# One token-ordered buffer for branch B's results, one load per merge, whole-tile loads of queries and keys, and earlier gate weights, in a hybrid encoder layer

## The chip, the cores and the metric

The kernel runs on one core of a Trainium2 chip. The metric is the device time of one execution in microseconds (us); lower is better. TensorE (PE) does the matmuls, VectorE (DVE), ScalarE (ACT) and GpSimd (POOL) the rest; SyncE (SP) and POOL issue the DMA transfers, which 16 DMA engines carry out. Everything is float32; a matrix product is made of several matmuls of high and low parts (`hi`, `lo`), so that TensorE is busy nearly all the time.

## The reference

1280 tokens (1024 of a sample, 256 of a prompt, as two sequences) pass through one encoder layer of width 1024, here with the RMS norms, reshapes and the final norm left out:

```python
z = h @ w_in                       # queries, keys, values of branches A and B, and 2 x 1024 gate logits
gates = sigmoid(z[..., o6:] + b_gate).reshape(b, S, 2, D_MODEL)
o_a = _banded_attention(qa, ka, va, 128, 1, rel_bias[:, :8], sink)     # 8 heads, 2 key heads
# branch B: three dilations (1, 4, 16), 4 heads each
for gi, (window, dil) in enumerate(B_GROUPS):
    o, lse = _banded_attention(_to_residues(qb), _to_residues(kb), _to_residues(vb), window // (2 * dil), dil, ...)
    outs.append(_from_residues(o, dil)); lses.append(_from_residues(lse, dil))
alpha = softmax(stack(lses), axis=0)          # over the three dilations, per token and head
o_b = sum(alpha[..., None] * stack(outs))
merged = gates[:, :, 0] * (o_a @ w_branch_a) + gates[:, :, 1] * (o_b @ w_branch_b)
x = x + merged @ w_out
return x + square(relu(rmsnorm(x) @ w_up)) @ w_down
```

A "residue" of a dilation `dil` is every `dil`-th token. The attention of a dilation runs over residues, so its results come out in residue order.

## The kernel before, in words

The tokens are 10 tiles of 128, 8 of the sample (`NS` = 1024 tokens) and 2 of the prompt (`NP` = 256). The kernel has stages one after the other: input projections, with branch B's attention woven in (to about 550 us); branch A's attention with the gate logits of the sample's leftovers and the prompt and with branch B's merge (about 555 to 706 us); branch projections, gating and output projection; the MLP. The change touches the end of the first and the whole of the second. Each engine runs its instructions in the order in which the program gives them (`manual_schedule`); nothing is reordered at run time, and an instruction that waits holds up all behind it on its engine. SP's list of DMAs, too, is in program order.

*Branch B's results.* `leave` (L580 to L603) copies an attention step's results, their negated maxima and their sums into rows of `ROW` = 132 numbers (528 bytes), and POOL's DMAs put them into three DRAM buffers, `scr_b[g]` for dilation `g`, ordered by residue. For each of the 10 merges (a pair of token tiles `t`, `t+1` and a head pair `i`), `load_rows` (L1142 to L1158) brings the rows of 256 tokens and three dilations into a tile `r` of 128 partitions; since the buffers are ordered differently and a merge wants the same tokens of all three, it takes 8 SP DMAs for a sample pair and 6 for a prompt pair. `alpha_steps` computes the softmax weights on DVE and ACT, `merge` the weighted sum on DVE, `turn_merged` transposes the result for the next product and puts the tokens back in order.

*Branch A.* A unit `u` (0 to 3) is a head pair. `load_unit(u)` loads keys (`kk`, the sample's, 4 KB a row; `kp`, the prompt's, 1 KB a row) for every second unit, and queries (`q`, and by `load_prompt` `qp`) for each. Keys and queries lie in DRAM with 64 rows for a head; the tile has them in both halves of the 128 partitions (`HALVES`): the keys twice the same, the queries two heads. Each half is a DMA of its own from 64 rows. The loop over 40 tiles `(u, t)` (written in pairs, `i` and `j`, at its call site) does for each: scores on PE into a bank `sc` (L1059, L1060), bias and maximum on DVE, exponentials on ACT, transposes, values on PE (`pv`, L1103), one or two steps of `fill` (gate logits, L191 on PE) and, by `merge_steps`, as many steps of the ten merges as keep `done[1]` at 50*(i+j-1)/35. Unit `u+1` is loaded when unit `u` starts. The rows of merge `n`+2 are loaded in the course of merge `n`.

*Gate weights.* `fetch` (L221) loads the next raw weight tile (`raw`, 512 KB), `prepare` splits it into `whi` (ACT) and `wlo` (DVE); the weights are consumed by `fill`. `entering` (L626 to L641) is a generator of which a step is done at each step of the last projections: it fetches the first raw tile, loads bias and unit 0, fetches the second raw tile, loads four parts of the normalized input that had been put by (`h21`: `hhi`, `hlo` from `scr_h`), and prepares the first weight. Among these on SP's list stand stores `scr_g<-z` of finished gate logits.

Of the kernel before, what the change touches and what calls it, by code (L numbers as in the profile page):

```python
# [10 lines left out]
F32 = mybir.dt.float32  # L11
# [85 lines left out]
def encoder_kernel(  # L97
# [28 lines left out]
    def slot(name, shape=(P, D), dt=F32):  # L126
        return slots.tile(list(shape), dt, name=name, tag="m", bufs=N_M)
# [90 lines left out]
    def fetch():  # L218
        src, shape, _ = specs[len(raws)]
        raws.append(wslot("raw", shape))  # L220
        nc.sync.dma_start(raws[-1], src)  # L221
# [49 lines left out]

    NH = AH + 3 * BH

    scr_b = [dram.tile([T, 2, ROW], F32, name=f"scr_b{g}_") for g in range(3)]
    scr_o = [dram.tile([P, AH * HD], F32, name=f"scr_o{t}") for t in range(NT)]
    scr_x = [dram.tile([P, D], F32, name=f"scr_x{t}") for t in range(NT)]

# [130 lines left out]

    shared = {}

    def load_unit(u):

        st = {}
        g = u // 2
        if u == 0:
            shared["kp"] = slot("kp", (P, 4, NP), F32R)
        if u % 2 == 0:
            kk = [slot("kk", (P, NS), F32R) for _ in range(2)]
            for i in range(2):
                for r in HALVES:  # L420
                    nc.sync.dma_start(kk[i][r, :].bitcast(F32), scr_ka[i, g, :, :NS])
                    nc.sync.dma_start(shared["kp"][r, 2 * g + i, :].bitcast(F32), scr_ka[i, g, :, NS:])
            shared["k"] = [Pair(kk[i], shared["kp"][:, 2 * g + i, :]) for i in range(2)]
        st["q"] = [Pair(slot("q", (P, NS), F32R), None) for _ in range(2)]
        for h in range(2):
            for a in range(2):
                nc.sync.dma_start(st["q"][h].s[HALVES[a], :].bitcast(F32), scr_qa[u][a, h, :, :NS])
        if u:
            load_prompt(u, st)
        else:  # L430
            shared["v"] = [slot("va", (P, 8, P)), None]
            nc.sync.dma_start(shared["v"][0],
                              scr_v[:NS, 512 : 512 + P].rearrange("(t p) c -> p t c", p=P))
        st["k"], st["v"] = shared["k"], shared["v"]
        return st

    def load_prompt(u, st):
        for h in range(2):
            st["q"][h].p = qslot("qp", (P, NP), F32R)
            for a in range(2):  # L440
                nc.sync.dma_start(st["q"][h].p[HALVES[a], :].bitcast(F32), scr_qa[u][a, h, :, NS:])
        if not u:
            shared["v"][1] = qslot("vp", (P, 2, P))
            nc.sync.dma_start(shared["v"][1], scr_v[NS:, 512 : 512 + P].rearrange("(t p) c -> p t c", p=P))
# [46 lines left out]
    def attention_b(make):  # L491
# [100 lines left out]
        def leave(j, pv, st):  # L592
            o = make("o", (P, 4, ROW), n=2)
            for b, (g, i, tiles) in enumerate(steps[j]):
                c, nt = 2 * b, len(tiles)
                if b == 0 or nt != len(steps[j][0][2]) or nt == 1:
                    m = 4 if b == 0 and nt == len(steps[j][1][2]) == 2 else nt
                    nc.scalar.activation(o[:, c : c + m, : 2 * HD],
                                         pv[:, P * c : P * (c + m)].rearrange("p (x c) -> p x c", c=P), AF.Copy)
                    nc.gpsimd.tensor_copy(o[:, c : c + m, 2 * HD :], st[:, c : c + m, :])  # L600
                for x, (t, (pieces, _, _)) in enumerate(tiles):
                    for p0, nq, qa, _ in pieces:
                        nc.gpsimd.dma_start(scr_b[g][qa : qa + nq, i, :], o[p0 : p0 + nq, c + x, :])  # L603

        load(0)
        yield
# [19 lines left out]
    def entering():  # L626

        nonlocal unit0
        fetch()
        yield  # L630
        bias0 = load_bias(0, wslot)
        yield
        unit0 = load_unit(0), bias0
        yield
        fetch()
        for i in range(2):
            h21[i] = slot("hhi", (P, 2, 512), F32R), slot("hlo", (P, 2, 512), F32R)
            for j in range(2):
                nc.sync.dma_start(h21[i][j].bitcast(F32), scr_h[i][:, j])
        prepare()  # L640
        yield  # L641

# [227 lines left out]
    if True:  # L870
# [157 lines left out]
            b, p = pair(b, p, PAIRS[j], PAIRS[j + 1] if j + 1 < len(PAIRS) else None, hooks, tick)  # L1028
        run(att_b)
        flush(True)  # L1030
    first_part.close()


# [2 lines left out]
    if True:  # L1036
# [101 lines left out]
        def load_rows(i, t):  # L1138

            r = rows_b[i, t] = slot("r", (P, 2, 3, ROW))  # L1142
            for j in range(2):
                if t < 8:
                    a = P // 8 * (t + j)
                    nc.sync.dma_start(r[:, j, 0, :], scr_b[0][P * (t + j) : P * (t + j + 1), i, :].rearrange(
                        "(q m) c -> m q c", m=8))
                    rows = scr_b[1][:NS, i, :].rearrange("(r q m) c -> m r q c", r=4, m=2)[:, :, a : a + 16]
                    for m in range(2):
                        nc.sync.dma_start(r[64 * m : 64 * m + 64, j, 1, :], rows[m])  # L1150
                    nc.sync.dma_start(r[:, j, 2, :], scr_b[2][:NS, i, :].rearrange(
                        "(r q) c -> r q c", r=8)[:, a : a + 16])
                    continue
                nc.sync.dma_start(r[:, j, 0, :], scr_b[0][P * (t + j) : P * (t + j + 1), i, :].rearrange(
                    "(q m) c -> m q c", m=2))
                for g in (1, 2):
                    nc.sync.dma_start(r[:, j, g, :], scr_b[g][NS:, i, :].rearrange(
                        "(r q) c -> r q c", r=2)[:, 64 * j : 64 * j + 64])  # L1158

        alphas = {}  # L1160

# [33 lines left out]
        def merges_of(seq):  # L1195
            load_rows(*seq[0])
            yield
            load_rows(*seq[1])
            for _ in range(5):
                yield  # L1200
            yield from alpha_steps(*seq[0])
            for n, x in enumerate(seq):
                now = merge(*x)
                next(now)
                coming = alpha_steps(*seq[n + 1]) if n + 1 < len(seq) else iter(())
                next(coming, None)
                yield
                next(now)
                yield
                if n + 2 < len(seq):  # L1210
                    load_rows(*seq[n + 2])
                next(now)
                yield
                next(coming, None)
                yield
# [5 lines left out]
    if True:  # L1221
# [5 lines left out]
        def turn_merged(t, tag="sc"):  # L1227

            if t in (0, 4, 8):
                ob_hi.block(t // 4)  # L1230
                ob_lo.block(t // 4)
            ps = bank(tag)
            for j in range(2):
                nc.tensor.transpose(ps[:, P * j : P * j + P], merged[t // 4][:, t % 4, P * j : P * j + P], ident)
            k = 8 if t < 8 else 2
            parts = []
            for j in range(2):
                hi, lo = (x.at(j, P * t, P).rearrange("p (q m) -> p q m", m=k) for x in (ob_hi, ob_lo))
                parts.append((hi, lo, ps[:, P * j : P * j + P].rearrange("p (m q) -> p q m", m=k)))
            banks_t["b", t] = parts  # L1240
            for hi, _, src in parts:
                nc.scalar.activation(hi, src, AF.Copy)
# [56 lines left out]
        for i in range(0, len(order) + 4, 2):  # L1299
            for j in range(2):  # L1300
                if i < len(order):
                    u, t = order[i + j]
                    if t == 0 and u < 3:
                        units[u + 1] = load_unit(u + 1), load_bias(u + 1, lambda name, shape: a3(name, shape, 2))
                    if i >= 36:
                        turn_merged(i + j - 36, "mm")
                    scores(u, t)
                    if j == 0 and i > 2:
                        values_of(*order[i - 4 : i - 2])
                    if i >= 36:  # L1310
                        weights_b = prepare_steps() if j == 0 else weights_b
                        next(weights_b, None)
                        low_b(i + j - 36)
                if i >= len(order) and j == 0:
                    values_of(*order[i - 4 : i - 2])
                if 0 < i < len(order) + 2:
                    transposes(*order[i + j - 2])
                if i < len(order):
                    exponentials(*order[i + j])
                merge_steps(i, j)  # L1320
                steps_of(fill, 2 if i > len(order) - 2 or j and i > 30 else 1)
            if i == 38:
                load_o(0)
                load_o(1)
# [602 lines left out]
```

## Time and profile before

| what | value |
|---|---|
| median of 3 runs (lowest to highest) | 1716.57 us (1714.93 to 1716.98) |
| the profiled execution | 1717.32 us, of which its span in the trace 1715.5 us |
| mean granted TensorE clock | 0.992 of full speed |
| PE busy in the span | 1679.1 us (98%) |
| DVE, ACT, POOL busy | 986.2 us (57%), 727.1 us (42%), 436.3 us (25%) |
| share of the 16 DMA engines taken by the hardware queue q1 / by POOL's software queue q0 | 42.3% / 4.3% |

How to read what follows: times are us from the span's start. "PE L1059 MATMUL sc<-kk,q" is a matmul of line 1059 that writes `sc` and reads `kk` and `q`. In brackets behind an instruction stands how long its engine had been idle and what released it. A view by stretches ("windows") gives for each stretch the busy time and the number of instructions of PE, its weight loads, DVE, ACT and POOL, then the granted clock, the busy share of the 16 DMA engines and GB/s.

### The profile page before, as it was taken

What the parts mean: (1) busy time and instruction counts of PE and PEld (TensorE: products, weight loads), DVE (VectorE), ACT (ScalarE), POOL (GpSimd) and SP (SyncE); (2) the same over time, 40 slices, a digit from 0 to 9 for tenths busy, and PEclk for the clock granted to TensorE, in tenths of its full rate; (3) what the DMA queues carried; (4) which work ended last, traced back from release to release, by engine and by line L of the source; (5) the groups of instructions that cost most, each with busy time, mean ns of one, the idle gap of its engine ahead of it and who ended that gap; (6) DMA issues with size and microseconds to landing.
All of it is one profiled execution on the core that took longest, in us unless ns stands there. A gap on an engine that the chain in (4) does not pass through costs nothing.

```text
span 1715.5 us, 26529 instructions
## 1 busy us (share of the span) xinstructions
PE 1679.1 (98%) x9952; PEld 1428.6 (83%) x9952; DVE 986.2 (57%) x1675; ACT 727.1 (42%) x1550; POOL 436.3 (25%) x401
## 2 busy tenths in 40 slices
PE   7999999999999988999999999999999999999998
PEld 6898888888887877888888888888887888888886
DVE  6734554554442566566568555554547776667575
ACT  6232543544442555635266433333334333333345
POOL 0210122121111121100100264555556332314140
PEclk9999999999999999999999999999999999999999
DMA  7315666664536752727012434443446844633333
GB/s 240 122 50 126 167 177 190 186 188 127 151 121 190 200 153 75 260 90 277 25 74 74 155 117 128 157 133 116 143 157 231 292 131 157 210 115 117 117 117 123
DMA packets 233624, 256.35 MB, mean 149 GB/s; under 512 B 30447, under 2 KB 164035, under 8 KB 233368
## 3 DMA queue, kind: packets, MB, share of 16 engines
q1 hardware_dynamic: 224024, 229.05, 42.3%
q0 software_dynamic: 8384, 23.51, 4.3%
q10 hardware_dynamic: 1088, 2.10, 0.3%
q8 instruction: 79, 1.29, 0.3%
q14 instruction: 49, 0.40, 0.1%
HBM read 169.10 MB, written 90.73 MB: 151 GB/s over the span
## 4 chain that ended last, share of the span: by engine, by line
PE 90%; DVE 3%; DMA 3%; SPq 1%; issue 1%; ACT 1%; POOL 0%; DVEq 0%; ACTq 0%; POOLq 0%
PE dn L349 21%; PE x L349 18%; PE mm L191 13%; PE z L349 9%; PE v L760 5%; PE mm L349 5%; PE pv L349 5%; PE y L349 5%; PE sc L541 1%; PE pv L587 1%; DMA r<-scr_b__84 1%; PE pt L566 1%; PE pv L1103 1%; PE tr L340 1%; PE pt L1086 1%
## 5 line engine op out<-in xcount | busy, mean ns | idle before, releaser
L349 PE MATMUL dn<-dhi,ulo 128*128 128x512 f32 x448 | 175.6, 392 | 3.4 <-DVE ulo L185 3.4
L349 PE MATMUL dn<-dlo,uhi 128*128 128x512 f32 x448 | 175.5, 392 | 0.0
L349 PE MATMUL dn<-dhi,uhi 128*128 128x512 f32 x448 | 175.4, 392 | 0.0
L349 PE MATMUL x<-chi,wlo 128*128 128x512 f32 x424 | 166.7, 393 | 0.0
L349 PE MATMUL x<-clo,whi 128*128 128x512 f32 x424 | 165.6, 391 | 0.0
L349 PE MATMUL x<-chi,whi 128*128 128x512 f32 x424 | 165.1, 389 | 0.0
L316 DVE TENSOR_TENSOR wlo<-ta,whi 128x1024 fp32r<-128x1024 f32 x30 | 55.2, 1839 | 160.9 <-ACT whi L314 160.9
L316 DVE TENSOR_TENSOR wlo<-raw,whi 128x1024 fp32r<-128x1024 f32 x60 | 89.2, 1487 | 89.7 <-ACT whi L314 89.7
L383 POOL TENSOR_TENSOR tb<-raw 128x512 f32<-128x512 f32 x16 | 20.8, 1300 | 338.4 <-DMA raw<-in_w_up_dram 191.1
L185 DVE TENSOR_TENSOR ulo<-uraw,uhi 128x1024 fp32r<-128x1024 f32 x56 | 97.2, 1754 | 13.2 <-ACT uhi L184 13.2
L349 PEld LDWEIGHTS dn<-dhi,ulo 128*128 128x128 f32 x448 | 84.8, 189 | 22.2 <-DVE ulo L185 4.7
L349 PEld LDWEIGHTS dn<-dhi,uhi 128*128 128x128 f32 x448 | 84.8, 189 | 17.8
L349 PEld LDWEIGHTS dn<-dlo,uhi 128*128 128x128 f32 x448 | 84.7, 189 | 17.5
L349 PEld LDWEIGHTS x<-chi,wlo 128*128 128x128 f32 x424 | 79.7, 188 | 17.2 <-issue 1.8
L349 PEld LDWEIGHTS x<-chi,whi 128*128 128x128 f32 x424 | 79.6, 188 | 17.0
L349 PEld LDWEIGHTS x<-clo,whi 128*128 128x128 f32 x424 | 79.8, 188 | 15.1 <-DVE clo L316 0.4
L1763 DVE TENSOR_TENSOR v<-v,dn 128x512 f32<-128x512 f32 x90 | 59.7, 682 | 43.4 <-PE dn L349 41.8
L1612 POOL TENSOR_TENSOR t<-raw,t 128x1024 f32<-128x1024 f32 x16 | 47.0, 2956 | 146.9 <-DMA raw<-in_w_down_dram 146.9
L551 DVE CUSTOM_DVE_ANT_0 s<-sc,bias 128x128 f32<-128x128 f32 (+1 forms) x120 | 36.3, 340 | 65.6 <-PE sc L541 65.6
L349 PE MATMUL dn<-dhi,up 128*128 128x512 f32 x224 | 73.5, 389 | 0.0
L349 PE MATMUL z<-chi,wlo 128*128 128x512 f32 x184 | 71.9, 391 | 0.0
L349 PE MATMUL z<-chi,whi 128*128 128x512 f32 x184 | 71.6, 389 | 0.0
(346 smaller groups left out, 4623.7 us busy)
## 6 DMA issues: line engine op xcount, KB each, us to landing
scr_u<-u SPq DMA_DIRECT2D x112, 320.0 KB
uraw<-scr_u SPq DMA_DIRECT2D x56, 512.0 KB
raw<-in_w_in_dram SPq DMA_DIRECT2D x33, 512.0 KB
raw<-in_w_up_dram SPq DMA_DIRECT2D x32, 512.0 KB
raw<-in_w_down_dram SPq DMA_DIRECT2D x28, 512.0 KB
sg<-scr_g SPq DMA_DIRECT2D x32, 256.0 KB
uraw<-scr_u SPq DMA_DIRECT2D x28, 256.0 KB
v<-scr_v SPq DMA_DIRECT2D x96, 64.0 KB
```

Source lines behind the costliest of these rows:

```text
L185: nc.vector.tensor_tensor(lo, src, hi.bitcast(F32), op=ALU.subtract)
L191: nc.tensor.matmul(ps, a, b, start=i == 0, stop=i == len(seq) - 1)
L316: nc.vector.tensor_tensor(lo, src, hi.bitcast(F32), op=ALU.subtract)
L340: nc.tensor.transpose(ps[:, P * i : P * (i + 1)], xn[t][:, P * k : P * (k + 1)], ident)
L349: nc.tensor.matmul(ps, a, b, start=first and i == 0, stop=last and i == len(seq) - 1, skip_group_check=True)
L383: eng.tensor_tensor(tb[:, 0], b12, b11, op=ALU.subtract)
L541: nc.tensor.matmul(ps[p0 : p0 + nq, c : c + W], qk[d, b, q : q + nq], qk[d, b, k : k + W], start=True, stop=True)
L551: nc.vector.tensor_tensor_reduce(d, src, bt, 1.0, -3.0e38, op0=ALU.add, op1=ALU.max, accum_out=m[:, h : h + 1])
L566: nc.tensor.transpose(ps[:, P * k : P * k + P], s[:, b, k % 2, P * (k // 2) : P * (k // 2) + P], ident)
L760: nc.tensor.matmul(ps[:, :n], a, b, start=k == 0 and j == 0, stop=k == KC - 1 and j == 2)
L1612: nc.gpsimd.tensor_tensor(o, a, b, op=ALU.subtract)
L1763: nc.vector.tensor_tensor(v, v, ps, op=ALU.add)
```

## The change

1. `scr_b` becomes one buffer `[T, 2, 3, ROW]` in token order. `leave` writes each piece with a stride (1, 4 and 8 rows for the three dilations in the sample, 1, 2 and 2 in the prompt); the number of POOL's DMAs, their sizes and their order stay.
2. `load_rows` is one DMA: for each partition and tile of the pair 396 consecutive numbers (three rows, 1584 bytes). The 76 DMAs of the ten merges become 10. `turn_merged` copies in order, since nothing is to be put back.
3. Keys and queries: one DMA for a tile of 128 partitions instead of one for each half. For the keys a leading dimension of 2 with stride zero (`twice`) reads the 64 rows two times; for the queries the leading dimension is the head. For all units together 48 DMAs become 24: `kk` and `kp` 16 become 8, `q` 16 become 8, `qp` 16 become 8.
4. `entering` fetches the second raw tile ahead of `load_unit(0)`; a third fetch and the four loads of `h21` move behind the last stores of gate logits (`flush(True)`).
5. The first `alpha_steps` stands one step earlier among the merge steps, and in the loop the merge steps stand ahead of the tile's exponentials.

```diff
-    scr_b = [dram.tile([T, 2, ROW], F32, name=f"scr_b{g}_") for g in range(3)]
+    scr_b = dram.tile([T, 2, 3, ROW], F32, name="scr_b")
...
+    def twice(x):
+        return x.unsqueeze(0).to_broadcast([2, *x.shape])
...
             for i in range(2):
-                for r in HALVES:
-                    nc.sync.dma_start(kk[i][r, :].bitcast(F32), scr_ka[i, g, :, :NS])
-                    nc.sync.dma_start(shared["kp"][r, 2 * g + i, :].bitcast(F32), scr_ka[i, g, :, NS:])
+                nc.sync.dma_start(kk[i].bitcast(F32), twice(scr_ka[i, g, :, :NS]))
+                nc.sync.dma_start(shared["kp"][:, 2 * g + i, :].bitcast(F32), twice(scr_ka[i, g, :, NS:]))
...
         for h in range(2):
-            for a in range(2):
-                nc.sync.dma_start(st["q"][h].s[HALVES[a], :].bitcast(F32), scr_qa[u][a, h, :, :NS])
+            nc.sync.dma_start(st["q"][h].s.bitcast(F32), scr_qa[u][:, h, :, :NS])
...
-            for a in range(2):
-                nc.sync.dma_start(st["q"][h].p[HALVES[a], :].bitcast(F32), scr_qa[u][a, h, :, NS:])
+            nc.sync.dma_start(st["q"][h].p.bitcast(F32), scr_qa[u][:, h, :, NS:])
...
-                        nc.gpsimd.dma_start(scr_b[g][qa : qa + nq, i, :], o[p0 : p0 + nq, c + x, :])
+                        base, n = (NS, NP) if qa >= NS else (0, NS)
+                        step = STEPS[g][base > 0]
+                        r, k = divmod(qa - base, n // step)
+                        first = base + r + step * k
+                        nc.gpsimd.dma_start(scr_b[first : first + step * (nq - 1) + 1 : step, i, g, :],
+                                            o[p0 : p0 + nq, c + x, :])
...
+        fetch()
         unit0 = load_unit(0), bias0
         yield
-        fetch()
-        for i in range(2):
-            h21[i] = slot("hhi", (P, 2, 512), F32R), slot("hlo", (P, 2, 512), F32R)
-            for j in range(2):
-                nc.sync.dma_start(h21[i][j].bitcast(F32), scr_h[i][:, j])
         prepare()
...
         flush(True)
+        fetch()
+        for i in range(2):
+            h21[i] = slot("hhi", (P, 2, 512), F32R), slot("hlo", (P, 2, 512), F32R)
+            for j in range(2):
+                nc.sync.dma_start(h21[i][j].bitcast(F32), scr_h[i][:, j])
...
-            for j in range(2):
...
-                nc.sync.dma_start(r[:, j, 0, :], scr_b[0][P * (t + j) : P * (t + j + 1), i, :].rearrange(
-                    "(q m) c -> m q c", m=2))
-                for g in (1, 2):
-                    nc.sync.dma_start(r[:, j, g, :], scr_b[g][NS:, i, :].rearrange(
-                        "(r q) c -> r q c", r=2)[:, 64 * j : 64 * j + 64])
+            nc.sync.dma_start(r.rearrange("p j g c -> p j (g c)"),
+                              scr_b[P * t : P * t + 2 * P, i].rearrange("(j p) g c -> p j (g c)", p=P))
...
-            for _ in range(5):
+            for _ in range(4):
                 yield
-            yield from alpha_steps(*seq[0])
+            coming = alpha_steps(*seq[0])
+            next(coming)
+            yield
+            yield
+            next(coming)
+            yield
...
+                merge_steps(i, j)
                 if i < len(order):
                     exponentials(*order[i + j])
-                merge_steps(i, j)
```

What this makes of SP's list is shown at two places. The first is the entry into branch A: the raw weights, unit 0, the last stores of gate logits and unit 1. In before (a row "x4" is four alike in a run):

```order
L221 DMA raw<-in_w_in_dram 128x8x128
L884 DMA scr_g_136<-z 128x512
L221 DMA raw<-in_w_in_dram 128x8x128
L639 DMA hhi<-scr_h_143 128x1024
L639 DMA hlo<-scr_h_143 128x1024
L639 DMA hhi<-scr_h_144 128x1024
L639 DMA hlo<-scr_h_144 128x1024
L884 DMA scr_g_137<-z 128x512
L884 DMA scr_g_137<-z 128x256
L221 DMA raw<-in_w_in_dram 128x8x128
L441 DMA qp<-scr_qa_110 64x256 x4
L444 DMA vp<-scr_v 128x2x128
```

and now, from the fetch that was moved up:

```order
L221 DMA raw<-in_w_in_dram 128x8x128
L423 DMA kk<-scr_ka 128x1x1024
L424 DMA kp<-scr_ka 128x1x256
L423 DMA kk<-scr_ka 128x1x1024
L424 DMA kp<-scr_ka 128x1x256
L428 DMA q<-scr_qa_108 128x1x1024 x2
L433 DMA va<-scr_v 128x8x128
L885 DMA scr_g_134<-z 128x512
L885 DMA scr_g_135<-z 128x512
L885 DMA scr_g_135<-z 128x256
L221 DMA raw<-in_w_in_dram 128x8x128
L1036 DMA hhi<-scr_h_141 128x1024
```

The second raw tile now stands ahead of unit 0's keys, the loads of `h21` behind the last stores, and the eight key loads of 64 rows and four query loads are four and two of the form 128x1x1024 and 128x1x256.

The second place is the end of the merges' loads, the prompt's. In before:

```order
L1154 DMA r<-scr_b__82 128x1x132
L1157 DMA r<-scr_b__83 128x1x132
L1157 DMA r<-scr_b__84 128x1x132
L1154 DMA r<-scr_b__82 128x1x132
L1157 DMA r<-scr_b__83 128x1x132
L1157 DMA r<-scr_b__84 128x1x132
L221 DMA raw<-in_w_branch_b_dram 128x2x512 x2
```

and now, from the load of unit 3:

```order
L1149 DMA r<-scr_b 128x2x396 x2
L428 DMA q<-scr_qa_111 128x1x1024 x2
L441 DMA qp<-scr_qa_111 128x1x256 x2
L1149 DMA r<-scr_b 128x2x396 x4
L221 DMA raw<-in_w_branch_b_dram 128x2x512 x2
```

Here each merge's six or eight rows are one row; four merges' loads stand behind unit 3's queries. PE's and POOL's lists are the same as before.

More of the change, by code (lines that the diff above doesn't have):

```diff
@@ L1142, in load_rows @@
             r = rows_b[i, t] = slot("r", (P, 2, 3, ROW))
-            for j in range(2):
[L1144 to L1154, printed above, removed]
-                    "(q m) c -> m q c", m=2))
-                for g in (1, 2):
-                    nc.sync.dma_start(r[:, j, g, :], scr_b[g][NS:, i, :].rearrange(
-                        "(r q) c -> r q c", r=2)[:, 64 * j : 64 * j + 64])
+            nc.sync.dma_start(r.rearrange("p j g c -> p j (g c)"),
+                              scr_b[P * t : P * t + 2 * P, i].rearrange("(j p) g c -> p j (g c)", p=P))
         alphas = {}
@@ L1234, in turn_merged @@
                 nc.tensor.transpose(ps[:, P * j : P * j + P], merged[t // 4][:, t % 4, P * j : P * j + P], ident)
[L1235 to L1239, printed above, removed]
+            parts = [(ob_hi.at(j, P * t, P), ob_lo.at(j, P * t, P), ps[:, P * j : P * j + P]) for j in range(2)]
             banks_t["b", t] = parts
```

## Prediction

> **What bounds the kernel now.** I read the page's head and its chain first, then the table of PE's waits, then the chain, the windows and SP's queue in the stretch that the change touches.
>
> ```profile
> span 1715.5 us, 26529 instructions
> PE 1679.1 (98%) x9952; PEld 1428.6 (83%) x9952; DVE 986.2 (57%) x1675; ACT 727.1 (42%) x1550; POOL 436.3 (25%) x401
> PE 90%; DVE 3%; DMA 3%; SPq 1%; issue 1%; ACT 1%; POOL 0%; DVEq 0%; ACTq 0%; POOLq 0%
> ```
>
> PE is the bound: 1679.1 of 1715.5 us busy, so all idle time of PE together is 36 us. No change of loads can gain more than that plus what a lowered clock costs. PE's waits (us in total, times, longest) name what of it lies here:
>
> ```profile
> PE sc L1059 <- DVE m L1061: 9.8, 5, 4.2
> PE mm L191 <- DVE wlo L233: 4.0, 1, 4.0
> ```
>
> The 4.0 us are the second raw weight tile, the 9.8 us are scores that wait for a bank `sc`. The chain shows the cause of each:
>
> ```profile
> 544.64 8.21 DMA raw<-in_w_in_dram
> 552.87 1.06 ACT whi L231
> 553.96 1.23 DVE wlo L233
> 555.24 11.29 PE mm L191 x48
> ...
> 595.21 8.50 DMA q<-scr_qa
> 606.12 2.52 DMA r<-scr_b__84
> 616.12 3.21 DMA r<-scr_b__84
> 632.12 3.83 DMA r<-scr_b__84
> 657.68 9.06 DMA r<-scr_b__84
> ```
>
> The weight was fetched at 544.64 and split 10.6 us later. The others are rows `r` of merges: a first alpha instruction on DVE waits for the last of eight loads, the tile's bias and maximum stand behind it, and the scores after next find no bank. How much that costs in all, clock included, the windows tell (us, PE, PEld, DVE, ACT, POOL busy, granted clock, DMA share, GB/s):
>
> ```profile
> 545.00:570.00 25.00, 21.01 (x107) 18.11 (x106) 5.30 (x15) 4.69 (x9) 2.92 (x5) 0.86 0.92 279
> 600.00:640.00 40.00, 34.91 (x374) 30.22 (x372) 26.92 (x112) 23.48 (x70) 8.80 (x16) 0.96 0.59 164
> 640.00:670.00 30.00, 25.28 (x290) 21.49 (x291) 19.55 (x83) 17.62 (x54) 4.82 (x9) 0.95 0.31 92
> ```
>
> PE is idle 3.99 + 5.09 + 4.72 = 13.8 us. The clock falls after each gap and costs about 0.14 x 25 + 0.04 x 40 + 0.05 x 30 = 6.6 us more. So 20.4 us are the most that the stretch has to give.
>
> **The change, part by part.** *Raw weight earlier, `h21` later.* The fetch moves ahead of unit 0 and then lands 8 us sooner; its 4.0 us gap and the slow 6 us behind it (clock 0.51) go, if nothing else is late at the scores that follow. `h21` now stands on the DMA queue behind unit 0.
>
> *One load for a merge's rows.* 76 DMAs become 10, and a merge's rows land as a whole. With unhindered queues the five score waits (9.8 us) and their clock go. PE and POOL get no instruction more. POOL's stores keep number, bytes and order; their rows of 528 bytes were gathered from scattered places by the loads and are now scattered by the stores, whose last issue and the first load of rows stand here:
>
> ```profile
> 532.00 1.05 POOL L603 DMA_DIRECT2D scr_b__82<-o  x2 [0.29 <-POOL o L600]
> ...
> 570.51 0.71 SPq L1146 DMA_DIRECT2D r<-scr_b__82  x1
> ```
>
> 38 us hide them, so I cost them at nothing; were a store 1 us slower nobody would see it. The alphas' exponentials now stand ahead of the tile's on ACT, which was busy 23.48 of 40 us, and the first alpha one step earlier on DVE needs merge 0's rows one tile (3 us) sooner: nothing either while rows are there, and while they are not, both are contained in the row waits below.
>
> *Keys and queries in whole tiles.* Here I expect the loss. A half was 64 rows to 64 partitions; the new load reads from 2 x 64 rows, as an access pattern whose slowest dimension is 2. This form stands in before at one place, the prompt's `r` rows (L1154 and L1157, source 2 x 64 x 132, also to 128 partitions). What they do:
>
> ```profile
> 640.74 0.50 SPq L1154 DMA_DIRECT2D r<-scr_b__82  x1
> 641.29 0.50 SPq L1157 DMA_DIRECT2D r<-scr_b__83  x1
> ...
> 644.67 1.72 SPq L1157 DMA_DIRECT2D r<-scr_b__83  x1
> ...
> 655.89 1.74 SPq L1157 DMA_DIRECT2D r<-scr_b__83  x1
> 657.68 2.43 SPq L1157 DMA_DIRECT2D r<-scr_b__84  x1
> ```
>
> The first issues take SP 0.50 us, then each takes 1.7 to 2.4: the queue is full. The hardware queue in 640 to 660 us (packets, MB, share of the 16 engines), and the window of its first half:
>
> ```profile
> q1 hardware_dynamic: 1215, 0.63, 12.6%
> ...
> 640.00:650.00 10.00, 10.00 (x132) 8.78 (x132) 8.62 (x36) 6.50 (x21) 2.00 (x4) 1.00 0.18 50
> ```
>
> 12.6% of 16 engines is 2.0 engines, all the time, while SP is held back. So twelve loads of 66 KB run on two engines, one after the other, and fourteen engines stand by; 657.68 + 9.06 = 666.74 is the landing of the last, so 12 x 67.6 kB take 26.0 us from the first issue, 31 GB/s. So I take two engines for `kk`, `kp`, `q` and `qp`.
>
> Beside this row stands the Trainium skill, "DMA: Bandwidth & Descriptors", section "Rules for kernel authors": an outermost dimension smaller than 16, a leading zero-stride broadcast among them, confines a whole DMA to at most that many engines. By that rule `twice` has two engines and so has the head dimension of the queries; the trace agrees, at 12.6%. The same section says not to bother with two transfers to disjoint partition halves, since they serialize, and to use one over 128 partitions; by that one the edit is right, and the time would be that of the first rival below. The trace bears out the first.
>
> What the loads weigh (KB each):
>
> ```profile
> q<-scr_qa SPq DMA_DIRECT2D x16, 256.0 KB
> qp<-scr_qa SPq DMA_DIRECT2D x16, 64.0 KB
> hhi<-scr_h SPq DMA_DIRECT2D x2, 512.0 KB
> ...
> 554.00:560.00 6.00, 4.76 (x11) 3.80 (x12) 1.51 (x2) 0.41 (x1) 1.09 (x2) 0.51 1.04 390
> ...
> q0 software_dynamic: 754, 2.23, 11.6%
> ```
>
> Now 4 `kk` and 8 `q` of 524 kB, 4 `kp` and 8 `qp` of 131 kB: 7.86 MB on two engines. Their rate is bounded below by the 31 GB/s of the 528-byte rows (254 us), above by `hhi` and `hlo`, whose 4-KB rows on all 16 make the 390 GB/s of 554 to 560, 24.4 GB/s an engine, 49 for two (160 us). The rows of `kk` and `q` are 4 KB too, so I take 160 us: a load of 64 rows an engine at 0.16 us is 10.3 us, the small ones 3.0. The other loads from here to the last rows of merge 6 (three raw tiles, `h21`, `va`, `vp`, seven `r`: about 8.3 MB) cost the two engines their sixteenth, 8.3/390 = 21 us. POOL's queue takes 11.6% of 537 to 600, and I count 10 us for it. About 10 us the queue stands empty, when a load waits for a buffer: `r` 3, 4 and unit 3's `q` wait for a merge or a tile that is itself late. The queue starts at about 537, after the raw tile, where unit 0 started:
>
> ```profile
> 535.78 0.53 SPq L421 DMA_DIRECT2D kk<-scr_ka  x1
> 566.36 0.28 PE L1059 MATMUL sc<-kk,q 128*128 128x256 f32 x1
> 639.83 0.33 PE L1059 MATMUL sc<-kk,q 128*128 128x384 f32 x1
> 651.92 0.28 PE L1059 MATMUL sc<-kp,qp 128*128 128x256 f32 x1
> 704.88 1.08 PE pv L1103 x32
> ```
>
> The first scores stood at 566.36, and without gap and slow clock would at about 560. Two keys, two prompt keys and two queries alone are 4 x 10.3 + 2 x 3.0 = 47 us, with the share of others 52: the second query lands at about 589, and PE, with nothing else in its order, stands for some 29 us. By the same stepping `h21` lands at 600 (7 us more), and unit 0's prompt queries and unit 1's queries (2 x 10.3 + 4 x 3.0 = 33 us, with others' share 38) go ahead of merge 0's rows, which land at 638: DVE's alpha waits, and PE stands about 24 us at the sixth tile. Unit 2's keys and queries (53 us with the prompt's, and others' share) stand ahead of merge 3's rows, 698, a stall of 35 us. Unit 3's `q` and `qp` ahead of merge 6's: landing at 537 + 160 + 21 + 10 + 10 = 738, with issue and landing 740. What remains then are 19 tiles. Four tiles without a wait took 651.92 - 639.83 = 12.09, 3.02 each, so 57 us, and the end of the loop is at 797 where it was 705. Stages behind it shift and do not change. That is +92 with the gains of the other parts already used up (without any wait the loop would end at 684). With a low clock after the last stall, +1: 1717.3 + 93 = 1810 against the profiled execution, which lies 0.7 above the median of the runs, so 1810 stands to it as well. SP's own saving, 24 + 66 issues of about 0.55 us, is 50 us of a queue that is not the limit when unblocked.
>
> **The rivals.**
> *All sixteen engines (faster).* If the loads of 2 x 64 rows spread like those of 64, units land as early as before, SP is 50 us shorter, raw and rows are in time: 1717.3 less the 20.4 is 1697. For it: the 64-row loads of `q` moved 223 GB/s at a DMA share of 1.04 in 544 to 548. Against: the prompt's rows, the only ones of that form. It decides if `q` lands within 4 us.
> *Only the first unit is late.* If two engines carry the loads, but later units' come while nobody waits, only the first stall counts: 29 us and 7 for `h21`, less the 20 gained: 1733. For it: a unit is loaded ten tiles ahead, 30 us. Against: a unit's queries are 2 x 13.3 us and with keys 53, and the rows of merges, wanted 15 us after, stand behind in the same queue.
> *Longer rows slower.* The `kk` and `q` halves of before took 16 x 4096/223e3 = 0.29 us a row. If this belongs to them and not to 64 partitions being written, 12 x 64 x 0.13 us = 100 us more: 1910. Against: 528 bytes take 0.029 us a row on two engines, and 4096 at the same rate per byte 0.22 at most; at 0.20 the stepping gives 1851.
> *No effect.* Gains and losses cancel only if two engines run at about three times `hhi`'s rate an engine, so that merge 6's rows land by 648.
>
> ```profile
> 544.00:548.00 4.00, 4.00 (x20) 3.30 (x19) 0.00 (x0) 0.00 (x0) 0.00 (x0) 1.00 1.04 223
> ```
>
> **How the numbers follow.** Two engines near `hhi`'s rate, which I predict: 0.78; all sixteen: 0.07; only the first unit: 0.04; slow rows: 0.10; no effect: 0.01. A run of this kernel is told from no change beyond some 0.2%, 3.4 us. Faster 0.07, same 0.01, slower 0.92. The predicted time is 1810. At 0.141 us a row the stepping gives 1787, at 0.176 1824, at 0.20 1851; fewer empty waits or 1/16 shares that cost less take 15 more off: 1770 below. Above I go to 1890, into the slow rows, since four stalls in chain can each run longer than stepped.
>
> **What would show it.** In the changed kernel: the first scores at about 590 and not 566, behind a wait of PE for `q` of some 25 to 30 us; `q` and `kk` with 10 us from one landing to the next and SP's issues of them held back 5 to 10 us each; between 540 and 740 a DMA share near 0.13 to 0.3 while SP is blocked, and the q1 share near two engines; stalls of PE on DVE's alpha at merges 0, 3 and 6; loop end near 797; from there everything as before. PE's gap on `wlo` at 551 gone shows the raw step right. I am wrong if `q` lands in 3 us or less, at a DMA share near 1.0.

## The result, and the profile after

The changed kernel takes 1816.47 us (median of 4 runs, 1814.4 to 1818.28) against 1716.78 us before (4 runs): 1.0582 times as long, 95% interval 1.0563 to 1.06. The profiled execution took 1817.22 us, its span 1815.4 us. The forecast was 1810, range 1770 to 1890.

One correction to the text ahead: the two halves of a query tile hold the high and the low part of one head's queries, not two heads. The leading dimension of 2 in their load is that of the parts; what the prediction derives from it is the same.

The page of the changed kernel: PE is as busy in microseconds as it was (1680.2 after 1679.1), over a span that is 100 us longer.

```profile
span 1815.4 us, 26393 instructions
PE 1680.2 (93%) x9952; PEld 1430.5 (79%) x9952; DVE 984.7 (54%) x1675; ACT 726.2 (40%) x1550; POOL 436.4 (24%) x401
```

Its waits of PE (what waits, for whom, us in total, times, longest):

```profile
PE sc L1065 <- DVE m L1067: 78.3, 4, 35.7
PE sc L1065 <- DMA q<-scr_qa: 28.9, 2, 19.3
PE mm L191 <- DMA hhi<-scr_h: 5.4, 1, 5.4
```

The wait on `wlo` is gone, as meant; the scores' wait for DVE has gone from 9.8 to 78.3 us, and there is a new one for the queries themselves. PE's order of time shows the five places (the first two rows are one place, unit 0's queries):

```profile
580.20 0.58 PE L1065 MATMUL sc<-kk,q 128*128 128x256 f32 x1 [19.32 <-DMA q<-scr_qa]
590.60 0.58 PE L1065 MATMUL sc<-kk,q 128*128 128x256 f32 x1 [9.61 <-DMA q<-scr_qa]
596.77 0.76 PE L191 MATMUL mm<-hhi,wlo 128*128 128x512 f32 x1 [5.38 <-DMA hhi<-scr_h]
639.92 0.58 PE L1065 MATMUL sc<-kk,q 128*128 128x256 f32 x1 [23.74 <-DVE m L1067]
700.87 0.69 PE L1065 MATMUL sc<-kk,q 128*128 128x384 f32 x1 [35.67 <-DVE m L1067]
745.72 0.69 PE L1065 MATMUL sc<-kk,q 128*128 128x384 f32 x1 [18.57 <-DVE m L1067]
```

The first two rows are unit 0's two queries, 10.4 us apart: that is the price of one load on the queue. The last three are scores behind the first alphas of merges 0, 3 and 6. DVE's row for merge 3 names what is really waited for, and it has PE standing behind it:

```profile
699.31 0.16 DVE L1159 TENSOR_TENSOR mm__6367<-r 128x4 f32<-128x4 f32 x1 [37.78 <-DMA r<-scr_b]
```

What the DMA engines do meanwhile, in 672 to 686 us, where no engine computes anything, stands in a window and in the line of the hardware queue (packets, MB, share of 16 engines):

```profile
672.00:686.00 14.00, 0.00 (x0) 0.00 (x0) 0.00 (x0) 0.00 (x0) 0.00 (x0) 0.50 0.13 51
```
```profile
q1 hardware_dynamic: 178, 0.72, 12.8%
```

Everything waits, and the hardware queue takes 12.8% of the sixteen engines, the work of two, at 51 GB/s. (The trace gives the share of all, not the engines by name.) SP is held back as the prompt's rows held it back before:

```profile
541.89 10.30 SPq L424 DMA_DIRECT2D kp<-scr_ka  x1
552.29 13.83 SPq L428 DMA_DIRECT2D q<-scr_qa  x2
...
688.04 3.84 SPq L1149 DMA_DIRECT2D r<-scr_b  x1
```

The loop of branch A, whose last values stood at 704.88, ends here:

```profile
807.79 1.08 PE pv L1109 x32
```

102.9 us later; the profiled executions differ by 99.9 us. So the whole loss lies in this stretch. The stages behind it took 1010.6 us in before and 1007.6 us here, from the start of the loop's last values to the end of the span; in the twelve kept traces this varies from 1006.0 (e6) to 1011.3 us (e5), in no order with the edits. A few microseconds between two single executions can come from there.

### The profile page after: what moved, and what is told of

Its sections match the earlier page's. It is cut to its first block, busy times and chain, and to the rows that moved or that the text cites. A ratio compares the mean times of both kernels' runs of the same rounds, so it can differ in the third digit from the quotient of the medians.

```text
span 1815.4 us, 26393 instructions
## 1 busy us (share of the span) xinstructions
PE 1680.2 (93%) x9952; PEld 1430.5 (79%) x9952; DVE 984.7 (54%) x1675; ACT 726.2 (40%) x1550; POOL 436.4 (24%) x401
## 4 chain that ended last, share of the span: by engine, by line
PE 87%; SPq 6%; DMA 3%; DVE 2%; issue 1%; ACT 1%; POOL 0%; DVEq 0%; ACTq 0%; POOLq 0%
PE dn L349 20%; PE x L349 17%; PE mm L191 14%; PE z L349 9%; PE v L761 5%; PE mm L349 5%; PE pv L349 4%; PE y L349 4%; SPq L441 3%; DMA r<-scr_b 2%; PE sc L541 1%; PE pv L587 1%; PE pt L1092 1%; PE pv L1109 1%; PE pt L566 1%
## 5 line engine op out<-in xcount | busy, mean ns | idle before, releaser
L1065 PE MATMUL sc<-kk,q 128*128 128x384 f32 (+1 forms) x64 | 23.9, 378 | 107.2 <-DVE m L1067 78.3
L607 POOL DMA_DIRECT2D scr_b<-o x72 | 39.0, 545 | 257.2 <-ACT o L598 202.2
L1065 PEld LDWEIGHTS sc<-kk,q 128*128 128x128 f32 x64 | 13.8, 215 | 110.4 <-DVE m L1067 79.8
L349 PEld LDWEIGHTS dn<-dhi,ulo 128*128 128x128 f32 x448 | 84.1, 188 | 20.4 <-DVE ulo L185 3.2
L185 DVE TENSOR_TENSOR ulo<-uraw,uhi 128x1024 fp32r<-128x1024 f32 x56 | 93.1, 1682 | 11.7 <-ACT uhi L184 11.7
```

The lines of the kernel that those rows point to most:

```text
L185: nc.vector.tensor_tensor(lo, src, hi.bitcast(F32), op=ALU.subtract)
L349: nc.tensor.matmul(ps, a, b, start=first and i == 0, stop=last and i == len(seq) - 1, skip_group_check=True)
L607: nc.gpsimd.dma_start(scr_b[first : first + step * (nq - 1) + 1 : step, i, g, :], o[p0 : p0 + nq, c + x, :])
L1065: nc.tensor.matmul(ps[:, :W], q, st["k"][1][:, P * lo : P * lo + W], start=True, stop=False)
```

## The experiments

Times are medians. The kernel before ran on the same chip each time, with medians of 1714.68 (e1 to e4), 1716.12 (e5 to e8) and 1717.07 us (e9, e10).

| run | edit in short | us | ratio to before, 95% interval | last values of the loop at |
|---|---|---|---|---|
| after | the change | 1816.47 | 1.0563 to 1.06 | 807.79 |
| e1 | change, loads in halves | 1692.92 | 0.9861 to 0.99 | 684.84 |
| e2 | change, whole loads, slowest dimension 64 | 1693.12 | 0.9859 to 0.9898 | 684.14 |
| e3 | before, whole loads only | 1839.36 | 1.0704 to 1.0742 | 830.75 |
| e4 | change, only keys whole | 1735.55 | 1.01 to 1.0136 | 725.99 |
| e5 | change, halves, slowest dimension 2 | 1819.04 | 1.0574 to 1.0605 | 808.27 |
| e6 | the same with 4 | 1740.93 | 1.0128 to 1.0154 | 731.90 |
| e7 | the same with 8 | 1704.11 | 0.9909 to 0.994 | 692.51 |
| e8 | before, fetch and `h21` moved only | 1713.37 | 0.9975 to 0.9994 | 704.70 |
| e9 | change, halves, slowest dimension 16 | 1693.31 | 0.9852 to 0.9881 | 683.55 |
| e10 | e1 without the move of fetch and `h21` | 1698.3 | 0.988 to 0.991 | 689.60 |

**e1, the loads in halves again.**

```diff
-                nc.sync.dma_start(kk[i].bitcast(F32), twice(scr_ka[i, g, :, :NS]))
+                for r in HALVES:
+                    nc.sync.dma_start(kk[i][r, :].bitcast(F32), scr_ka[i, g, :, :NS])
```

and alike for `kp`, `q`, `qp`.

> The changed kernel, with kk, kp, q and qp loaded in two halves of 64 rows as before (24 DMAs more on SP); everything else of the change stays. Theory (the loss is the two engines to which the whole-tile form confines a load): PE has no wait for q and the row waits of merges 0, 3 and 6 go; the loop ends at 682 to 690 us, time 1697 to 1702. Rival A (the single row load, the scattered stores or the later h21 delay the merges and the first tiles): the landings stay late and the time stays above 1780. Rival B (fewer SP DMAs are a gain by themselves): 24 issues of 0.58 us come back on a path that waits, some 1705 to 1710.

1692.92 us: the loss is gone, and what remains of the change is a gain of 1.2%. The loop's end, 684.84, is where it was expected; the time is 4 us below the expected 1697 to 1702, which were reckoned from before's profiled execution (1717.3; beside e1 before's median is 1714.68). Rival A, that the row load, the scattered stores or the later `h21` bring the delays, falls.

**e2, whole loads with another slowest dimension.** The 24 saved DMAs stay saved; only the order of the rows on the partitions differs.

```diff
     def twice(x):
-        return x.unsqueeze(0).to_broadcast([2, *x.shape])
+        return x.unsqueeze(1).to_broadcast([HD, 2, x.shape[-1]])
...
-            nc.sync.dma_start(st["q"][h].s.bitcast(F32), scr_qa[u][:, h, :, :NS])
+            nc.sync.dma_start(st["q"][h].s.bitcast(F32), scr_qa[u][:, h, :, :NS].rearrange("a d t -> d a t"))
```

> The changed kernel, with as many DMAs as it has, the same bytes and rows, but the 128 partitions hold row d of both halves next to each other (partition 2d+a instead of 64a+d) for keys and queries alike, so that the access pattern's slowest dimension is 64 and not 2. Theory (the slowest dimension sets the number of engines): 16 engines, loads land like those of 64 rows, time 1697 to 1702. Rival A (one DMA that reads a row twice, or one of 128 partitions with 4-KB rows, is slow by itself): q lands near 590 again, time 1800 or more.

1693.12 us, as far below the expected 1697 to 1702 as e1, and for the same reason. A load that reads each row twice, with stride zero, is not slow by itself; nor is one of 128 partitions. PE's waits of this kernel in the stretch, all of them:

```profile
PE sc L1065 <- DVE m L1067: 1.4, 2, 1.1
```

and its windows at the start of the loop and where the changed kernel stood still:

```profile
540.00:560.00 20.00, 20.00 (x125) 18.00 (x124) 1.65 (x2) 4.19 (x6) 2.35 (x4) 1.00 1.07 372
600.00:640.00 40.00, 39.67 (x470) 35.47 (x470) 32.53 (x135) 27.28 (x84) 9.30 (x17) 1.00 0.53 163
```

In the first the same DMA list moves 372 GB/s, at a share of 1.07. e1 and e2 differ by 0.2 us: 24 issues on SP more or less make no difference in this kernel.

**e3, the whole loads alone, in the kernel before.** Its edit is the part of the change on `kk`, `kp`, `q` and `qp`.

> The kernel before with nothing but the whole-tile loads of kk, kp, q and qp. Theory: they alone bring the loss, and before's raw weight fetched behind unit 0 and its 76 row loads lose more than in the changed kernel, since they stand in the same queue: 1820 to 1850. Rival (the loss comes of the combination: h21, the third raw tile and whole rows behind the keys): 1740 or less.

1839.36 us, more than the whole change loses. The second raw tile, which is fetched behind unit 0 there, becomes the longest wait but one:

```profile
PE sc L1059 <- DVE m L1061: 94.2, 5, 46.6
PE mm L191 <- DVE wlo L233: 41.8, 1, 41.8
```

So the other parts of the change are worth some 23 us beside the slow loads (1839.36 to 1816.47; taken each against the runs of before beside it, 124.7 and 99.7, it is 25.0), about as much as without them (21.8 us, before to e1).

**e4, the keys alone whole.** As e1, with `kk` and `kp` left as changed.

> The changed kernel with q and qp in halves of 64 rows, and only kk and kp of units 0 and 2 by the whole-tile form: 53 us of two engines in place of 160. Theory, by the same stepping: unit 0's second query lands near 571, PE waits about 12 us there and 7 for h21, and some 7 us at merge 3; loop end near 710 to 720, time 1723 to 1735. Rival (zero stride, two reads of one row, is what is slow, so keys carry most of the loss): above 1770. Rival (only the queries matter): within 5 us of 1700.

1735.55 us, half a microsecond above what was expected. PE's two long waits are

```profile
PE sc L1067 <- DVE m L1069: 16.3, 2, 16.0
PE sc L1067 <- DMA q<-scr_qa: 14.3, 2, 13.0
```

The queries' wait is 14.3 us where 12 were stepped, the wait at merge 3 is 16.0 us where 7 were stepped. Keys that are a third of the bytes bring 43 of 124 us. Neither rival holds: zero stride is not what is slow, and the queries aren't alone.

**e5, e6, e7 and e9, the number of engines as a dose.** All have e1's DMAs, bytes and rows; only the order of the 64 rows of a half changes, keys and queries alike.

```diff
-                    nc.sync.dma_start(kk[i][r, :].bitcast(F32), scr_ka[i, g, :, :NS])
+                    nc.sync.dma_start(kk[i][r, :].bitcast(F32), scr_ka[i, g, :, :NS].rearrange("(d x) t -> x d t", x=4))
```

with x = 2, 4, 8 and 16.

> The changed kernel with halves of 64 rows as in e1, but within each half the rows are taken in the order of a pattern (2, 32, n), keys and queries alike (the product sums over the partitions, so their order is free). Number of DMAs, bytes and row lengths are e1's; only the slowest dimension is 2. Theory (engines = slowest dimension): two engines, the same 160 us of loads as in the changed kernel, time 1805 to 1825. Rival (e1 is fast because it has halves, or because each row is read by one transfer only once): 1693 to 1700.

> As e5, with a pattern (4, 16, n). Theory: four engines, loads of 80 us in all. By the stepping used for the prediction with half the price of a load: q lands near 565, row waits of some 7 us at merges 0 and 3 and 4 at merge 6, the loop ends 30 us later than without waits: 1723, and as the stepping came out up to 10 us short for two engines, 1720 to 1735. Rival (any order of rows that isn't contiguous is slow): as e5.

> As e5, with a pattern (8, 8, n). Theory: eight engines, 40 us of loads, which by the same stepping nobody waits for: 1692 to 1698. Rival (any order of rows that isn't contiguous is slow): as e5.

> The control of e5 to e7: halves with rows in the order of a pattern (16, 4, n). Theory (the slowest dimension alone): sixteen engines, as e1, 1692 to 1697. Rival (the order of the rows costs something beside the number of engines, which would explain why e7 took 1704): 1700 or more.

1819.04, 1740.93, 1704.11 and 1693.31 us. The hardware queue's line (packets, MB, share of 16 engines) is, for x = 2 in 672 to 686 us, for x = 4 in 540 to 548, for x = 8 in 540 to 546 and for x = 16 in 540 to 544, each a window in which SP's loads under way are all but wholly keys and queries:

```profile
q1 hardware_dynamic: 184, 0.72, 12.8%
```
```profile
q1 hardware_dynamic: 331, 0.70, 25.0%
```
```profile
q1 hardware_dynamic: 408, 0.96, 52.1%
```
```profile
q1 hardware_dynamic: 454, 0.93, 106.8%
```

That is the work of two, four, eight and sixteen engines (the share is a sum of packet times, so above 100% these overlap). The number of engines follows the slowest dimension of the pattern and nothing else that was varied; that rows are out of order costs nothing (e9 is as fast as e1, so e7's 11 us are put down to eight engines, not to the order). The sizes for four and eight engines were stepped too small: 1723, at most 1735, for 1741, and no loss, at most 1698, for 1704.

**e8, the raw weight and `h21` alone, in the kernel before.** Its edit is the part of the change in `entering` and behind `flush(True)`.

> The kernel before with only the raw weight fetched ahead of unit 0 and h21 with the third raw tile behind the last stores. Theory: the 4.0 us gap on wlo goes and with it some 3 us of a clock at half speed; the five row waits stay: 1706 to 1709 on a before of 1714.7. Rival (h21, later by 10 us and behind the stores, is late in its turn): 1712 or more.

1713.37 us, a ratio of 0.9975 to 0.9994: the theory expected two to three times that gain (5.7 to 8.7 us). Its waits and, in the chain, the last rows' load and the loop's end say why:

```profile
PE sc L1060 <- DVE m L1062: 13.9, 6, 6.2
```
```profile
657.26 9.05 DMA r<-scr_b__84
...
704.70 1.08 PE pv L1104 x32
```

The gap on `wlo` is gone, but the row waits have grown from 9.8 to 13.9 us, and the last values start 0.2 us earlier than before. The last rows land at 666.3 where it was 666.7, and PE, 6.5 us earlier at the first scores (559.85 for 566.36), waits for them that much longer. `h21` is not late, so the rival falls as well. The 2.7 us of the median are not in this stretch; they are not explained. (In the two traces the stages behind the loop took 1006.4 us after 1010.6, within the spread named above.)

**e10, the rows alone.** e1 with the two parts of e8 undone.

> The changed kernel with halves (as e1) and with before's order of the raw weight and h21 (fetch behind unit 0, h21 right after it): of the change there remain the token-ordered buffer, the one load for a merge's rows and the earlier alpha. Theory: the row waits (9.8 us) and their clock go, the 4.0 us gap on wlo and its half-speed clock stay: 1699 to 1704 on a before of 1716. With e8 (2.7 us) and e1 (some 22 to 23 us) this tells whether the two parts add up: if the raw weight's 7 us are real but were given back to row waits in e8, then this one lies 5 to 8 us above e1. Rival (the parts simply add): e1 plus 2.7 us, 1695 to 1697.

1698.3 us, just below the expected 1699 to 1704, against e9's 1693.31 on the same chip: the moved fetch and `h21` are worth 5.0 us once rows come early, as the loops' ends show (689.60 to 683.55). Its only wait left in the stretch besides 0.3 us is

```profile
PE mm L191 <- DVE wlo L233: 4.0, 1, 4.0
```

So the parts don't add: alone the early weight gives 0.2 us in the stretch, with the early rows 5 to 6.

What of the rows' edit brings its gain (18.8 us, before to e10 on the same chip) was not separated. It makes 76 loads 10, but it also changes their slowest dimension: by the source patterns in `load_rows` this was 8 and 4 for the sample and 2 for the prompt, and is 128 now. In before the sample's loads leave SP mostly at 0.58 us each, so there their number may count. The prompt's twelve, after the first three, are held back 1.6 to 2.4 us each on the work of two engines, as the changed kernel's keys and queries are.

e1, e2 and e9 are the fastest kernels of the study, 1.2 to 1.3% below before, and not told apart by their times. Of the three, e2 has 24 DMAs fewer.

## Why the prediction was right, point by point

**Two engines.** The step from the prompt's rows to the new loads held: a share of 12.8% after 12.6%. The Trainium skill's rule ("DMA: Bandwidth & Descriptors", section "Rules for kernel authors"), that the outermost dimension caps the engines, agrees with e5, e6, e7 and e9 at 2, 4, 8 and 16. The Trainium skill's advice in the same section, one transfer of 128 partitions over two halves, made no difference here where the slowest dimension was 64 (e1 and e2, 0.2 us apart), and with a slowest dimension of 2 it lost 124 us (after, against e1).

**The price of a row.** 49 GB/s were taken from `hhi`, against 31 from the 528-byte rows; 51 GB/s were measured. A query load was put at 10.3 us and took 10.4. (524 kB at 49 GB/s would be 10.7 us; the sum of 160 us goes by 49 GB/s, the stepping by a rounded 0.16 us a row.) That choice, by row length and not by form, decided the size of the forecast.

**The places.** The stepping put unit 0's second query at 589, PE's wait for the queries at 29 us, `h21`'s at 7 us, and those at merges 0 and 3 at 24 and 35 us. Measured were 590.6, 28.9, 5.4, 23.74 and 35.67. For merge 6 the prediction gave the landing of the rows, 740, and no wait; the wait was 18.57 us.

**What was mis-sized.** The end of the loop was put at 797 and came at 807.8. Merge 6's rows came 4 us later than stepped: DVE's first instruction on them,

```profile
744.30 0.16 DVE L1159 TENSOR_TENSOR mm__6769<-r 128x4 f32<-128x4 f32 x1 [20.23 <-DMA r<-scr_b]
```

stands at 744.3 for 740. Two errors cancel in part here. The slow loads, 7.86 MB at the measured 51 GB/s, take 154 us where 160 were set down; that leaves 53 us from 537 to 744.3 for all the rest, where 43 were set down (21 + 10 + 10, and 2 for issue and landing). The three terms were not measured one by one, and the first doesn't follow from its list: the loads named there come to 7.2 MB and not 8.3, 18 us and not 21. The tiles that remain took 807.79 - 745.72 = 62 us and not 57: their price of 3.02 us was taken at 640 to 652, where a tile has one step of gate logits, but late tiles have two for every second tile. Four of them here,

```profile
776.90 0.33 PE L1065 MATMUL sc<-kk,q 128*128 128x384 f32 x1
...
791.53 0.36 PE L1065 MATMUL sc<-kk,q 128*128 128x256 f32 x1
```

take 3.66 us each. In the 62 us lies also what the clock cost behind the last wait, 3 us (0.80 over 15 us) where 1 was set down:

```profile
745.00:760.00 15.00, 14.28 (x142) 12.70 (x143) 11.78 (x48) 9.59 (x30) 2.92 (x6) 0.80 0.26 75
```

Together the loop's end was 10.8 us late against the forecast, and 6.5 show in the time (1816.5 for 1810). The forecast time had 1 us for the clock beside the 797. And the stages behind the loop were 3 us shorter than in before's trace (102.9 at the loop's end, 99.9 in the profiled execution), a difference as it is found between single executions: these 3 us of the hit are luck.

**The gains.** 20.4 us were said to be the most that the stretch has to give. The loops of e1, e2 and e9 end 20.0, 20.7 and 21.3 us earlier than before's, so this held within a microsecond; their times gained 21.8, 21.6 and 23.8 us, and what is more than the stretch gave does not show in it. That the loop without waits ends at 684 came out to the microsecond (e2, 684.14). The scattered stores of `scr_b` cost nothing that e1 or e10 shows. SP's saved issues were said to be off the path: true for the 24 of the keys and queries (e1 against e2). For the rows' 66 no run tells it apart: in e8 the last rows land only 0.4 us earlier though PE comes 6.5 us sooner, but whether SP's issues or the engines of the old patterns hold them is not separated. What they cost are the row waits, which the sum counted under the rows.

**The rivals.** All sixteen engines is what e2 is, at 1693 for 1697, but by another slowest dimension. Only the first unit late falls: three of the five places, with 78 of 112 us, are later. Slower rows fall at 51 GB/s.

Not tried: the merges' rows issued ahead of the next unit's loads. How much of the 78 us is the rows' place in the queue behind slow loads, and could be had without making these fast, stays open.

## What to carry to other kernels

Before two half loads are joined into one, look at the slowest dimension of the source's access pattern, the one that was varied here: a leading 2, real or a zero-stride copy, gave the whole load the work of two of sixteen DMA engines (12.8%), and what stood behind it in the queue waited with it. The profile shows this as a DMA share of an eighth (0.13) while the issuing engine is held back for as long as a load takes. If the order of rows is free, as it is in a contraction, take the one that puts a large dimension outermost; and judge a wait's removal together with the wait that comes next, since an earlier start alone may only wait longer.

## What was not expected of the hardware

Eight engines still lost 11 us (e7 against e9; the profiled execution of e7 is the fastest of its four and 6.7 us behind e9's), though their loads came to 40 us by the same prices and nobody was to wait. The waits of e7 show that what stands behind them in the queue was late, `h21` and the first rows:

```profile
PE sc L1068 <- DVE m L1070: 2.9, 3, 1.8
...
PE mm L191 <- DMA hlo<-scr_h: 1.7, 2, 1.1
PE mm L191 <- DMA hhi<-scr_h: 1.6, 1, 1.6
```

These are 6.2 us, and its loop ends 9.0 us after e9's. Four engines cost 48 us (e6 against e9) where the stepping with halved prices gave 30.

The prices did not halve. From the queue lines above, 0.72 MB in 14 us, 0.70 in 8, 0.96 in 6 and 0.93 in 4 are 51, 88, 160 and 232 GB/s: 26, 22, 20 and 15 an engine, for two, four, eight and sixteen. So all loads of keys and queries, 7.86 MB, take an estimated 90 us on four engines and not 80, 49 on eight and not 40. This accounts for a part of what e6 and e7 lost beyond the stepping; why an engine moves less when more of them work was not tested.
